# Three two by two pairs in place of two in the first half of a channel mixer, on one Trainium2 core

## The chip, the cores and the metric

The kernel runs on one core of one Trainium2 chip. The metric is the device time of one execution in microseconds, as the median of a few runs of the same kernel. Three runs of the kernel before gave a median of 690.75 us (690.72 to 690.81). The profile is one further execution of that kernel, with its own time.

A core has a matrix engine (TensorE, PE in the profile, with its weight loads in a row of their own, PEld), a vector engine (VectorE, DVE), a scalar engine (ScalarE, ACT), a general engine (GpSimd, POOL) and a queue engine (SyncE, SP) that here only issues transfers. Each engine works through its own list of instructions in order, and semaphores tie the lists together.

## What is computed

The reference is one layer of a hybrid block on 512 positions of width 1024, in float32:

```python
h = rms_norm(x, norm_mix_g);  proj = h @ w_in
# gated short convolution, attention with forgetting, two gates, then
x = x + (g_conv * y_conv + g_attn * y_attn) @ w_o
h = rms_norm(x, norm_ffn_g)
up = causal_dwconv(h @ w_up, conv_ffn_w)      # 1024 -> 2 x 2816, three taps along the positions
a, b = split(up)
x = x + (silu(a) * b) @ w_down                # 2816 -> 1024
return rms_norm(x, norm_f_g)
```

The change lies in `h @ w_up` and its three taps, the channel mixer's way up.

## The kernel before

**Number format.** Each float32 factor is split into a high part and the rest (`wh`, `wl` for weights, `x1h`, `x1l` for the mixer's input), both in a rounded format that TensorE takes at one pass each. A product is three passes: high by high, rest by high, high by rest. Splitting a weight chunk is one copy on ScalarE (L279) and one subtraction on VectorE (L283). `split` does it, and `chunk` hands the next split chunk to the matmuls. Two high and two rest buffers are in use in turn, so a chunk can be split while the one before it is multiplied.

**The mixer in two halves.** The hidden width of 2816 is 22 pairs j of 128 columns of `a` and 128 of `b`. `PHASES` cuts them into a first half (j = 0 to 11) and a second (12 to 21). Each half first computes its pairs (`up`), then multiplies the products by its rows of `w_down` (`down`, L330, tiles `dn`).

**A direct pair** is two blocks (`block`), each 8 slices of the contraction by 3 passes by 2 halves of the positions, 48 matmuls of 256 positions. Its tiles are `p_up`, in one PSUM bank per block; block 2j is `a`, block 2j + 1 is `b`.

**A two by two pair** (`up_pair`, the j in `UPS`) computes both blocks at once with the Strassen-Winograd scheme: seven products of blocks of 128 by 128 in place of eight. Four partial sums lie in four banks, the tiles `us`. Its 84 matmuls take their weights in two steps, each a chunk `P` (768 columns, the plain weights) and a chunk `F` (1024 columns, the weight sums). After them VectorE adds the partial sums up (L1099 to L1104) and scales them by the inverse norm (L1127, L1125).

**Weight sums.** The `F` chunks are sums of weight blocks that transfers make on the chip before they are needed: `group` lists six transfers for a group of two steps, copies on SyncE's queue (L140) and adding transfers on GpSimd's queue (L143), each waiting for the one before. `tick` issues the next of them; `ticks` says how many per split chunk, and `MIXED` says how many groups are interleaved, copy by copy and add by add. The tiles are `sum`. GpSimd's list holds these adds in line with its multiplications.

**After a pair.** `tapped` runs the three taps on each block (one step on ScalarE, L615, two on VectorE, L616 and L619, tiles `fu`; three buffers in turn). `glu` applies SiLU (L1147) and multiplies on GpSimd: an even j gives `ge` (L1150), an odd one `go` (L1157). Both of a couple (2q, 2q + 1) together are then turned into four further sums (L1167 to L1172) and split (L1176 on ScalarE, L1177 on VectorE, tiles `gh`, `gl`) for `down`. These last pieces are queued in `later` and let out behind the splits of later chunks.

**Order.** In the second half the taps of a two by two pair are held (`held_up`) until the next block is multiplied and its successor chunks are split; in the first half they follow the pair at once. `after_split` is the scheduler's constraint that puts an operation behind the latest splits. PSUM banks are handed out by `ring`, a fixed circle of eight numbers; `down` uses the sets X = (6, 7, 0, 1) and Y = (2, 3, 4, 5).

Of the kernel before, what the change touches and what calls it, by code (L numbers as in the profile page):

```python
# [40 lines left out]
PHASES = ((0, 12), (12, NP))  # L41
# [11 lines left out]
)  # L53
GS = 2
NFF = len(STEPS[0]) + len(STEPS[1])
UPS = (3, 7, 12, 15, 18)
NUP = NFF + 2 * (8 - GS)
MIXED = (4, 2, 4, 4, 2, 4, 2)

PLAIN = [(m, k) for m in (6, 7) for k in range(*PHASES[1])]  # L60
PCUTS = (0, 4, 12, 20)
# [3 lines left out]
def block_kernel(ctx, tc, xT, vecs, wv, win, wmix, wo, wup, wst, wdp, outT):  # L65
# [13 lines left out]
    def bank(i, name):  # L79
        return ps.tile([P, S], F32, tag=f"b{i}", name=name)  # L80

    def ring(*ids):
        st = [0]

        def f(name):
            st[0] += 1
            return bank(ids[(st[0] - 1) % len(ids)], name)

        return f
# [32 lines left out]
    for (j0, j1), n0, n1 in zip(PHASES, (0, len(STEPS[0])), (len(STEPS[0]), NFF - 1)):  # L122
        groups += [[NUP + 2 * i, NUP + 2 * i + 1] for i, j in enumerate(UPS) if j0 <= j < j1]
        groups += [list(range(n, min(n + 2, n1))) for n in range(n0, n1, 2)]
    groups.append([NFF - 1])
    nstep = [len(d) for d in STEPS[0] + STEPS[1]] + [2] * (2 * (KB - GS) + 2 * len(UPS))
    todo = []
# [26 lines left out]
    i0 = 0  # L154
    for n in MIXED:
        todo += [op for ops in zip(*map(group, range(i0, i0 + n))) for op in ops]
# [11 lines left out]
    def up_n(j):  # L168
        return [NUP + 2 * UPS.index(j) + d for d in range(2)]

# [13 lines left out]
    n = 0  # L184
    for ph, (j0, j1) in enumerate(PHASES):
        for j in range(j0, j1):
            if j in UPS:
                for m in up_n(j):
# [13 lines left out]
    def after_split():  # L202

        st = ExitStack()
        for ins in order.values():
            st.enter_context(tc.issue_after(ins))
        return st
# [35 lines left out]
    def ticks(nm):  # L243

        if nm[0] in "iw":
            return 2 if nm in ("wo2", "wo4", "wo6") else 1
        if nm[0] == "m":
            return 2
        if nm[0] == "u":
            n = int(nm[2:])  # L250
            return 2 if n > 4 and n % (4 if n >= 2 * PHASES[1][0] else 2) != (3 if n >= 2 * PHASES[1][0] else 1) else 1
        return int(nm[0] == "F" and (int(nm[1:]) % 2 == 1 or int(nm[1:]) >= NUP))

    def split(hl=None):

        k = len(parts)
        if k == len(stream):
            return
        nm, _, ncol = stream[k]
        load(k + (LOOK if k >= gs0 else AHEAD))  # L260
        if k >= gs0:
            for _ in range(ticks(nm)):
                tick()
        if hl is None:
            hl = []
            for x in "hl":
                if k == 0:
                    wp.tile([P, PADW[x]], F32, tag=f"pad{x}", name=f"pad_{x}")
                hl.append(wp.tile([P, D], F32R, tag=f"w{x}", name=f"w{x}_{nm}", bufs=2)[:, :ncol])
        hi, lo = hl  # L270
        raw = raws[k]
        if k < 2:
            if k:
                keep(nc.scalar.activation(hi[:, :VW], raw[:, :VW], AF.Copy))
            else:
                keep(nc.vector.tensor_copy(hi[:, :VW], raw[:, :VW]))
            keep(nc.vector.tensor_copy(hi[:, VW:], raw[:, VW:]))
        else:
            ins = nc.scalar.activation(hi, raw, AF.Copy)  # L279
            order["hi"] = ins.ins  # L280
            if k < KB:
                keep(ins)
        ins = nc.vector.tensor_sub(lo, raw, hi.bitcast(F32))  # L283
        order["lo"] = ins.ins
        if k < KB:
            keep(ins)
        held[0] -= 1
        parts.append((hi, lo))
        run_later(k, 0.45 if nm[0] in "PF" and int(nm[1:]) >= NUP else {"u": 1.7, "P": 1.6, "F": 0.75, "d": 0}.get(nm[0], 3.5))
# [446 lines left out]
    n = 4 * H  # L736
# [59 lines left out]
    acc, bank_s, bank_t = ring(2, 0, 1), ring(3, 4), ring(5, 6)  # L796
# [12 lines left out]
    n = len(units)  # L809
# [21 lines left out]
    acc = ring(3, 4, 5, 6, 0, 1, 2, 7)  # L831
# [137 lines left out]
    def block(name, xh, xl, lead=False):  # L969
        wh, wl = chunk(name)  # L970
        q = acc(f"p_{name}")
        for kb in range(KB):
            ks = slice(kb * P, (kb + 1) * P)
            if lead and kb < 2:
                if kb:
                    passes([
                        (q[:, cs], 0, wh[:, b], wl[:, b], xh[:, a, cs], xl[:, a, cs], True, False)
                        for a, b in enumerate((slice(0, P), ks)) for cs in halves
                    ], 4)
                continue  # L980
            mm3(q, wh[:, ks], wl[:, ks], xh[:, kb, :], xl[:, kb, :], kb == 0, kb == KB - 1)
        return q
# [50 lines left out]
    xf_last.pop()()  # L1033
    nc.vector.tensor_sub(n2[1], ssq2, n2[0].bitcast(F32))
    xf_last.pop()()
    acc = ring(0, 1, 4, 5, 6, 7, 2, 3)
    nrm = {}

    def mid():
# [33 lines left out]
    def fz(name):  # L1073
        fz.n += 2
        a = 2 * KB + fz.n % (2 * KB)
        return xg[:, a : a + 2].rearrange("p h c -> p (h c)")
# [11 lines left out]
    def up_pair(j):  # L1088

        nonlocal xg, x1  # L1090
        flush([("xf", q) for q in range(4)])
        p23, p45, p16, p7 = banks = [acc(f"us{j}{i}") for i in range(4)]
        pair(up_n(j), x1_form, banks)
        z = fp.tile([P, S], F32, tag="fu", name=f"uz{j}", bufs=3)
        u = fp.tile([P, S], F32, tag="fu", name=f"uu{j}", bufs=3)[:, : S // 2]
        lo, hi = halves
        with after_split():
            nc.scalar.activation(z[:, lo], p16[:, lo], AF.Copy)
            nc.vector.tensor_add(z[:, hi], p16[:, hi], z[:, lo])  # L1099
            nc.vector.tensor_add(u, p7[:, lo], z[:, hi])  # L1100
            nc.vector.tensor_add(z[:, hi], p45[:, hi], z[:, hi])
            nc.vector.tensor_add(p23, p23, z)
            p45h = p45.rearrange(halves_of, h=2)
            nc.vector.tensor_add(p45h, p45h, u.unsqueeze(1).to_broadcast([P, 2, S // 2]))  # L1104
        if j == UPS[-1]:
            xg = xfp.tile([P, 4 * KB, 2 * P], F32, tag="xf", name="xg")
            x1 = xg[:, : 2 * KB].rearrange(whole, h=2)
            for a in range(0, KB, 4):
                nc.gpsimd.dma_start(x1[:, a : a + 4, :], x1d[:, a : a + 4, :])
        return p23, p45  # L1110

    def up(ph, j, rb2, pu=None):
        uu = []
        if j in UPS:
            pu = up_pair(j)
        for s_ in range(2):
            p = pu[s_] if pu else block(f"up{2 * j + s_}", x1h, x1l, True)
            if s_ == 0 and held_up:
                while len(parts) < chunk.n + 2:
                    split()  # L1120
                with after_split():
                    held_up.pop()()
            z = p if j <= UPS[-1] else fz(f"fz{j}{s_}")
            if s_ and j in UPS:
                nc.vector.scalar_tensor_tensor(z, p, -1.0, rb2, op0=ALU.mult, op1=ALU.mult)  # L1125
            else:
                nc.vector.tensor_mul(z, p, rb2)  # L1127
            if j not in UPS or not ph:
                z = tapped(j, s_, z)
            uu.append(z)  # L1130
        if j in UPS and ph:
            held_up.append(lambda: glu(ph, j, [tapped(j, s_, z) for s_, z in enumerate(uu)]))
        else:
            glu(ph, j, uu)
# [3 lines left out]
    def tapped(j, s_, z):  # L1138
        u = fp.tile([P, S], F32, tag="fu", name=f"fu{j}{s_}", bufs=3)
        taps(u, z, CF + 3 * (2 * j + s_))  # L1140
        return u
# [171 lines left out]
    for ph, (j0, j1) in enumerate(PHASES):  # L1313
        if ph:
            flush()
            acc = ring(*X, *Y)
        for j in range(j0, j1):
            up(ph, j, nrm["b"], None if j else pu)
        down(ph, ph * len(STEPS[0]))
# [212 lines left out]
```

## Time and profile before

| | |
|---|---|
| median of 3 runs | 690.75 us (690.72 to 690.81) |
| the profiled execution | 690.7 us, span 688.9 us |
| granted TensorE clock | 0.998 |
| TensorE busy | 680.0 us, 99% of the span, 5916 matmuls |
| VectorE busy | 547.3 us, 79% |
| ScalarE busy | 364.6 us, 53% |
| GpSimd busy | 184.2 us, 27% |
| first half, way up | 344.9 to 466.7 us |
| first half, way down | 466.7 to 523.8 us |
| second half, way up | 523.8 to 629.7 us |

Times in the views are microseconds from the span's start. The span is what the profiler saw from the first instruction to the last; the execution's own time is 1.8 us longer. Matmuls are pipelined, so the mean time of one (276 ns) is longer than the distance from one to the next; that distance is read from the chain of work that ended last, which lists a stretch of matmuls with its length and count.

### The profile page before, as it was taken

Reading aid. Unit: us, or ns where it says so; the run is one execution under the profiler, and the core shown is the slowest. Engines: PE = TensorE matmul, PEld = TensorE weight load, DVE = VectorE, ACT = ScalarE, POOL = GpSimd, SP = SyncE. Lnnn points to the kernel's source line nnn. Section 1 sums busy time; section 2 is a strip of 40 time slices with the busy share of each in tenths; the row PEclk is TensorE's granted clock in tenths of the full one; section 3 lists DMA queues with packets and bytes.
Section 4 is the critical chain, followed back from the end, with each engine's and each line's share of the span. In section 5 each row is a group of like instructions: output and inputs, shape, how many; then the busy total and the mean of one; then the engine's idle time right before and its main releaser. Section 6 shows DMA issues by size and latency. Waiting matters only on the chain.

```text
span 688.9 us, 14690 instructions
## 1 busy us (share of the span) xinstructions
PE 680.0 (99%) x5916; PEld 677.8 (98%) x5916; DVE 547.3 (79%) x864; ACT 364.6 (53%) x581; POOL 184.2 (27%) x209
## 2 busy tenths in 40 slices
PE   9999999999999999999999999999999999999996
PEld 8999999999999999999999999999999999999996
DVE  6677777886687877768987989987665889999885
ACT  6575556554564544446654635545444445456563
POOL 5123745444021010233502141330131322222000
PEclk9999999999999999999999999999999999999999
DMA  8626957478579797888985859679799987674623
GB/s 295 208 89 217 198 154 174 100 184 167 131 221 279 214 262 197 240 270 281 213 225 133 227 119 293 156 216 253 219 290 309 251 193 183 187 239 132 188 78 123
DMA packets 66117, 139.64 MB, mean 203 GB/s; under 512 B 5856, under 2 KB 30432, under 8 KB 65792
## 3 DMA queue, kind: packets, MB, share of 16 engines
q1 hardware_dynamic: 44592, 105.72, 46.7%
q0 software_dynamic: 20736, 32.28, 26.9%
q8 instruction: 46, 0.75, 0.4%
q10 hardware_dynamic: 720, 0.69, 0.3%
q14 instruction: 23, 0.19, 0.1%
HBM read 132.32 MB, written 49.81 MB: 264 GB/s over the span
## 4 chain that ended last, share of the span: by engine, by line
PE 89%; DVE 6%; ACT 2%; issue 2%; DMA 1%; ACTq 0%; POOL 0%; SPq 0%; DVEq 0%; POOLq 0%
PE p_up L312 18%; PE p_in L312 14%; PE dn L330 13%; PE gs L330 8%; PE p_wo L312 6%; PE us L330 6%; PE p_up L330 6%; PE yc L330 3%; PE ya L312 3%; PE o L705 2%; PE pa L524 2%; PE pb L526 1%; PE tp L690 1%; PE pdB L312 1%; PE pdA L312 1%
## 5 line engine op out<-in xcount | busy, mean ns | idle before, releaser
L143 POOL DMA_DIRECT2D sum<-in_wst_dram x66 | 70.8, 1163 | 122.3 <-DMA sum<-sum 93.0
L312 PE MATMUL p_in<-xf,wh_in 128*128 128x256 f32 x576 | 95.7, 278 | 0.0
L312 PE MATMUL p_up<-x1h,wh_up 128*128 128x256 f32 x416 | 81.1, 276 | 0.0
L312 PEld LDWEIGHTS p_in<-xf,wh_in 128*128 128x128 f32 x576 | 80.4, 188 | 0.7
L312 PE MATMUL p_up<-x1l,wh_up 128*128 128x256 f32 x416 | 81.0, 276 | 0.0
L312 PE MATMUL p_up<-x1h,wl_up 128*128 128x256 f32 x416 | 80.9, 276 | 0.0
L279 ACT ACTIVATE wh_F<-raw_F 128x1024 fp32r<-128x1024 f32 (+1 forms) x42 | 44.2, 1052 | 66.7 <-PE dn L330 26.2
L283 DVE TENSOR_TENSOR wl_F<-raw_F,wh_F 128x1024 fp32r<-128x1024 f32 (+1 forms) x42 | 53.4, 1272 | 28.8 <-ACT wh_F L279 28.5
L312 PEld LDWEIGHTS p_up<-x1h,wh_up 128*128 128x128 f32 x416 | 62.7, 188 | 0.0
L312 PEld LDWEIGHTS p_up<-x1l,wh_up 128*128 128x128 f32 x416 | 62.6, 188 | 0.0
L312 PEld LDWEIGHTS p_up<-x1h,wl_up 128*128 128x128 f32 x416 | 62.5, 188 | 0.0
L312 PE MATMUL p_in<-xf,wl_in 128*128 128x256 f32 x288 | 56.6, 278 | 0.1
L279 ACT ACTIVATE wh_up<-raw_up 128x1024 fp32r<-128x1024 f32 x34 | 36.0, 1057 | 38.2 <-PE p_up L312 27.9
L279 ACT ACTIVATE wh_P<-raw_P 128x768 fp32r<-128x768 f32 (+1 forms) x42 | 35.1, 836 | 36.4 <-PE dn L330 15.9
L283 DVE TENSOR_TENSOR wl_P<-raw_P,wh_P 128x768 fp32r<-128x768 f32 (+1 forms) x42 | 40.2, 956 | 12.5 <-ACT wh_P L279 6.8
L283 DVE TENSOR_TENSOR wl_up<-raw_up,wh_up 128x1024 fp32r<-128x1024 f32 x34 | 42.3, 1246 | 7.6 <-ACT wh_up L279 7.6
L312 PEld LDWEIGHTS p_in<-xf,wl_in 128*128 128x128 f32 x288 | 43.5, 188 | 0.3 <-DVE wl_in L283 0.3
L1150 POOL TENSOR_TENSOR ge<-fu,fu 128x512 f32<-128x512 f32 x11 | 20.2, 1832 | 67.5 <-DVE fu L619 34.0
L330 PE MATMUL dn<-gh,wh_F 128*128 128x256 f32 x156 | 36.4, 276 | 0.0
L330 PE MATMUL dn<-gl,wh_F 128*128 128x256 f32 x156 | 36.3, 276 | 0.0
L283 DVE TENSOR_TENSOR wl_in<-raw_in,wh_in 128x1024 fp32r<-128x1024 f32 x24 | 30.2, 1258 | 6.1 <-ACT wh_in L279 6.0
L279 ACT ACTIVATE wh_in<-raw_in 128x1024 fp32r<-128x1024 f32 x24 | 25.3, 1056 | 10.8 <-issue 3.4
(361 smaller groups left out, 2106.0 us busy)
## 6 DMA issues: line engine op xcount, KB each, us to landing
raw_F<-sum SPq DMA_DIRECT2D x41, 512.0 KB, 5.4
raw_up<-in_wup_dram SPq DMA_DIRECT2D x34, 512.0 KB, 5.9
raw_P<-in_wst_dram SPq DMA_DIRECT2D x41, 384.0 KB, 4.8
raw_in<-in_win_dram SPq DMA_DIRECT2D x24, 512.0 KB, 3.6
sum<-in_wst_dram POOLq DMA_DIRECT2D x41, 256.0 KB, 6.3
sum<-in_wst_dram SPq DMA_DIRECT2D x20, 512.0 KB, 8.7
sum<-in_wst_dram POOLq DMA_DIRECT2D x20, 512.0 KB, 9.6
sum<-sum SPq DMA_DIRECT2D x40, 256.0 KB, 5.7
```

The lines of the kernel that those rows point to most:

```text
L143: return lambda: keep(nc.gpsimd.dma_start(dst, src, accum_op=ALU.add))
L279: ins = nc.scalar.activation(hi, raw, AF.Copy)
L283: ins = nc.vector.tensor_sub(lo, raw, hi.bitcast(F32))
L312: keep(nc.tensor.matmul(out[:, cs], w, x[:, cs], start=start and i == 0 and c == 0, stop=stop and i == 2 and c == len(cut) - 1,))
L330: keep(nc.tensor.matmul(out, wl if x == 1 else wh, xl if x == 2 else xh, start=opens and bk not in seen, stop=closes and bk not in left,))
L524: keep(nc.tensor.matmul(pa[t][:, :VW], xt, w[:, :VW], start=start, stop=stop))
L526: keep(nc.tensor.matmul(pb[t], xt, w[:, VW:], start=start and t % 2 == 0, stop=stop and t % 2 == 1))
L690: keep(nc.tensor.transpose(tp[:, ks], pt[:, ks], ident))
L705: keep(nc.tensor.matmul(o[:, os_], vv[:, kb, pr, e, :], x[:, kb, cs], start=e == 0 and kb == 0 and i == 0, stop=e == 1 and kb == nk - 1 an ...
L1150: keep(nc.gpsimd.tensor_mul(ge, a.rearrange(halves_of, h=2), b.rearrange(halves_of, h=2)))
```

## The change

The first half gets three two by two pairs, j = 3, 6 and 9, in place of 3 and 7. The second half keeps 12, 15 and 18. There is one weight group more (23 in place of 22), so the interleaving `MIXED` and the number of ticks per chunk are other. The taps of the first half's two by two pairs are held like the second half's. The circle of PSUM banks for the first half puts banks 2 and 3 ahead of 6 and 7.

```diff
-UPS = (3, 7, 12, 15, 18)
+UPS = (3, 6, 9, 12, 15, 18)
 NUP = NFF + 2 * (8 - GS)
-MIXED = (4, 2, 4, 4, 2, 4, 2)
+MIXED = (4, 2, 4, 5, 2, 3, 3)
...
         if nm[0] in "iw":
-            return 2 if nm in ("wo2", "wo4", "wo6") else 1
+            return 2 if nm in ("wo0", "wo2", "wo4", "wo6") else 1
...
             n = int(nm[2:])
-            return 2 if n > 4 and n % (4 if n >= 2 * PHASES[1][0] else 2) != (3 if n >= 2 * PHASES[1][0] else 1) else 1
+            return 2 if n > 2 and n % 4 != 3 else 1
...
-    acc = ring(0, 1, 4, 5, 6, 7, 2, 3)
+    acc = ring(0, 1, 4, 5, 2, 3, 6, 7)
...
-            if j not in UPS or not ph:
+            if j not in UPS:
                 z = tapped(j, s_, z)
             uu.append(z)
-        if j in UPS and ph:
+        if j in UPS:
             held_up.append(lambda: glu(ph, j, [tapped(j, s_, z) for s_, z in enumerate(uu)]))
```

How the lists of instructions stand at three places follows. A row is line, operation, output<-inputs and shape; the number behind a tile's name is the pair and block, the couple q, or the weight group, and the one behind the underscore is the program's own.

First, VectorE behind pair 3 (`fu30`, `fu31` are its taps, `fu40` the taps of the next block, `wl_up10` and `wl_up11` the rests of chunks to come). Before:

```order
L1125 SCALAR_TENSOR_TENSOR us31_4983<-us31_4983,rb_n2_4660 128x512
L1127 TENSOR_TENSOR p_up8_5133<-p_up8_5133,rb_n2_4660 128x512
L616 SCALAR_TENSOR_TENSOR fu30_5117<-us30_4982,vec_64,fu30_5117 128x511
L283 TENSOR_TENSOR wl_up10_5256<-raw_up10_5041,wh_up10_5255 128x1024
L619 SCALAR_TENSOR_TENSOR fu30_5117<-us30_4982,vec_64,fu30_5117 128x510
L616 SCALAR_TENSOR_TENSOR fu31_5122<-us31_4983,vec_64,fu31_5122 128x511
L616 SCALAR_TENSOR_TENSOR fu40_5183<-p_up8_5133,vec_64,fu40_5183 128x511
L619 SCALAR_TENSOR_TENSOR fu31_5122<-us31_4983,vec_64,fu31_5122 128x510
```

Now:

```order
L1125 SCALAR_TENSOR_TENSOR us31_4987<-us31_4987,rb_n2_4662 128x512
L1127 TENSOR_TENSOR p_up8_5122<-p_up8_5122,rb_n2_4662 128x512
L283 TENSOR_TENSOR wl_up10_5188<-raw_up10_5045,wh_up10_5187 128x1024
L616 SCALAR_TENSOR_TENSOR fu30_5191<-us30_4986,vec_64,fu30_5191 128x511
L616 SCALAR_TENSOR_TENSOR fu31_5195<-us31_4987,vec_64,fu31_5195 128x511
L619 SCALAR_TENSOR_TENSOR fu30_5191<-us30_4986,vec_64,fu30_5191 128x510
L619 SCALAR_TENSOR_TENSOR fu31_5195<-us31_4987,vec_64,fu31_5195 128x510
L616 SCALAR_TENSOR_TENSOR fu40_5203<-p_up8_5122,vec_64,fu40_5203 128x511
```

The rest of chunk up10 now stands ahead of all four tap steps of pair 3.

Second, GpSimd in the last third of the first half's way up (`go4` is the product of pair 9, `ge4` of pair 8, `ge5` of pair 10; `sum14` is the group of pair 12 before, `sum15` that of pair 15 before and of pair 12 now, `sum16` that of pair 15 now). Before:

```order
L1157 TENSOR_TENSOR go3_5668<-fu70_5654,fu71_5659 128x512
L1150 TENSOR_TENSOR ge4_5786<-fu80_5720,fu81_5781 128x512
L143 DMA sum14_98<-in_wst_dram 256x1x256
L143 DMA sum15_99<-in_wst_dram 256x1x256
L1157 TENSOR_TENSOR go4_5924<-fu90_5850,fu91_5915 128x512
L143 DMA sum14_98<-in_wst_dram 256x1x256
L1150 TENSOR_TENSOR ge5_6054<-fu100_5984,fu101_6049 128x512
```

Now:

```order
L1157 TENSOR_TENSOR go3_5673<-fu70_5614,fu71_5668 128x512
L143 DMA sum15_99<-in_wst_dram 256x1x512
L143 DMA sum16_100<-in_wst_dram 256x1x512
L1150 TENSOR_TENSOR ge4_5792<-fu80_5725,fu81_5787 128x512
L143 DMA sum15_99<-in_wst_dram 256x1x256
L143 DMA sum16_100<-in_wst_dram 256x1x256
L143 DMA sum15_99<-in_wst_dram 256x1x256
L143 DMA sum16_100<-in_wst_dram 256x1x256
L1157 TENSOR_TENSOR go4_6012<-fu90_6003,fu91_6007 128x512
L1150 TENSOR_TENSOR ge5_6074<-fu100_6015,fu101_6069 128x512
```

All three adds of two groups now lie between `go3` and `go4`. Before, `go4` stood behind the second add of both, and the first adds stood ahead of `go3`.

Third, VectorE ahead of the way down (`wl_P0` is the rest of the first chunk of `down`; `go4` with L1168 to L1172 are the further sums of pairs 8 and 9, `gl` their rests). Before:

```order
L616 SCALAR_TENSOR_TENSOR fu101_6049<-p_up21_5999,vec_64,fu101_6049 128x511
L1177 TENSOR_TENSOR gl_4720<-go4_5924,gh_4719 128x512
L619 SCALAR_TENSOR_TENSOR fu101_6049<-p_up21_5999,vec_64,fu101_6049 128x510
L1177 TENSOR_TENSOR gl_4720<-go4_5924,gh_4719 128x512
L1127 TENSOR_TENSOR p_up22_6068<-p_up22_6068,rb_n2_4660 128x512
L283 TENSOR_TENSOR wl_P0_6192<-raw_P0_5926,wh_P0_6191 128x768
```

Now:

```order
L619 SCALAR_TENSOR_TENSOR fu101_6069<-p_up21_6019,vec_64,fu101_6069 128x510
L1168 TENSOR_TENSOR go4_6012<-go4_6012,ge4_5792 128x256
L1127 TENSOR_TENSOR p_up22_6076<-p_up22_6076,rb_n2_4662 128x512
L1171 SCALAR_TENSOR_TENSOR go4_6012<-go4_6012 128x256
L1177 TENSOR_TENSOR gl_4722<-ge4_5792,gh_4721 128x256
L1172 SCALAR_TENSOR_TENSOR go4_6012<-go4_6012 128x256
L616 SCALAR_TENSOR_TENSOR fu110_6126<-p_up22_6076,vec_64,fu110_6126 128x511
L1177 TENSOR_TENSOR gl_4722<-go4_6012,gh_4721 128x512
L619 SCALAR_TENSOR_TENSOR fu110_6126<-p_up22_6076,vec_64,fu110_6126 128x510
L1177 TENSOR_TENSOR gl_4722<-go4_6012,gh_4721 128x512 x2
L283 TENSOR_TENSOR wl_P0_6208<-raw_P0_5908,wh_P0_6207 128x768
```

The further sums of pairs 8 and 9 and all four of their rests now stand between the taps of block 21 and `wl_P0`; before, `wl_P0` came right behind the last of these rests, with the further sums well ahead of them.

## The prediction

> **What bounds the kernel now.** I read the page's busy times first, then what TensorE waits for, then the chain of work that ended last.
>
> ```profile
> span 688.9 us, 14690 instructions
> PE 680.0 (99%) x5916; PEld 677.8 (98%) x5916; DVE 547.3 (79%) x864; ACT 364.6 (53%) x581; POOL 184.2 (27%) x209
> ```
>
> TensorE is busy for 99% of the span: time can only be won by fewer matmuls or by ending one of its few waits. Its waits, all of them:
>
> ```profile
> PE warm L108 <- DVE ones L100: 1.1, 1, 1.1
> PE us L330 <- DVE wl_P L283: 0.9, 1, 0.9
> PE pa L524 <- ACT wh_v L274: 0.4, 1, 0.4
> ```
>
> Two belong to the start. The third, 0.9 us (name, total, times, longest), is a two by two pair that waits for VectorE's rest of its first chunk, `wl_P`. The chain (start, length, what, count) shows where that is:
>
> ```profile
> 366.02 1.36 PE p_up L330 x12
> 367.38 4.08 PE p_up L312 x36
> 371.46 9.52 PE us L330 x84
> ...
> 413.62 9.52 PE us L330 x84
> ...
> 466.67 57.12 PE dn L330 x504
> ...
> 588.65 8.45 PE us L330 x72
> ```
>
> The first half runs from pair 3 (371.46) into `down` (466.67) without a gap. The wait ends at 588.65, where only 72 of 84 matmuls follow: it stands in pair 18, behind its 12 matmuls with the high part.
>
> **The change, part by part.**
>
> *Matmuls.* A block of 48 takes 1.36 + 4.08 = 5.44 us, 0.1133 each; a two by two pair of 84 takes 9.52, also 0.1133 each. A direct pair is two blocks, 10.88 us. One more pair is changed over: 12 matmuls and **1.36 us** less.
>
> *Work of the other engines.* The stage's totals (columns: stretch, its length, busy of PE, PEld, DVE, ACT, POOL, clock, DMA share):
>
> ```profile
> 344.90:466.70 121.80, 121.80 (x1076) 121.80 (x1076) 105.56 (x148) 60.89 (x87) 33.63 (x26) 1.00 0.75 196
> 523.80:629.70 105.90, 104.96 (x926) 104.76 (x926) 95.52 (x136) 52.53 (x77) 30.33 (x27) 1.00 0.77 212
> ```
>
> ```profile
> L283 DVE TENSOR_TENSOR wl_up<-raw_up,wh_up 128x1024 fp32r<-128x1024 f32 x18 | 21.9, 1215 | 3.7 <-ACT wh_up L279 3.7
> L283 DVE TENSOR_TENSOR wl_F<-raw_F,wh_F 128x1024 fp32r<-128x1024 f32 x4 | 6.6, 1650 | 1.7 <-ACT wh_F L279 1.7
> L283 DVE TENSOR_TENSOR wl_P<-raw_P,wh_P 128x768 fp32r<-128x768 f32 x5 | 4.7, 950 | 0.2 <-DMA raw_P<-in_wst_dram 0.2
> L1102 DVE TENSOR_TENSOR us<-us,uz 128x512 f32<-128x512 f32 x2 | 1.4, 700 | 0.1
> L1099 DVE TENSOR_TENSOR uz<-us,uz 128x256 f32<-128x256 f32 x2 | 0.8, 418 | 0.0
> ```
>
> VectorE gets two `wl_P` and two `wl_F` for two `wl_up`, 2 x 0.95 + 2 x 1.65 - 2 x 1.22 = 2.8 us, and five additions, three like L1099 and two like L1102, 2.7: some 5.5 us more. It was idle for 121.8 - 105.6 = 16.2 us there, so on average this hides behind the matmuls; without that cover it would cost up to 5.5. ScalarE idles half the stage. The extra weight group is 1 MB of copies and 1 MB of adds in a stage whose transfer share is 0.75; by the table of ticks the last add of any group now comes at least 6 chunks before its chunk is loaded. I cost these at nothing, as I do the other bank circle: four banks per two by two pair and four per two direct pairs close the circle of eight, so `down`'s first set, (6, 7, 0, 1), is last used by pair 9, whose taps end before its product can start, 9 us before `down` by the model below.
>
> *Spacing.* What matters is when VectorE falls behind. Pairs 3, 6, 9 and then `down` (four blocks between each) have the spacing of 15 and 18 in the second half, held taps included, so that stretch is the model for the new one:
>
> ```profile
> 563.46 0.42 DVE L1167 TENSOR_TENSOR go<-ge 128x256 f32<-128x256 f32 x1
> ...
> 564.93 1.22 DVE L283 TENSOR_TENSOR wl_up<-raw_up,wh_up 128x1024 fp32r<-128x1024 f32 x1
> ...
> 566.39 0.68 DVE L1177 TENSOR_TENSOR gl<-ge,gh 128x512 fp32r<-128x512 f32 x1
> ...
> 579.86 0.75 DVE L616 SCALAR_TENSOR_TENSOR fu<-p_up,vec,fu 128x511 f32<-128x511 f32 x1 [0.26 <-ACT fu L615]
> ...
> 580.86 0.74 DVE L619 SCALAR_TENSOR_TENSOR fu<-p_up,vec,fu 128x510 f32<-128x510 f32 x1
> ...
> 582.11 1.22 DVE L1168 TENSOR_TENSOR go<-go,ge 128x256 f32<-128x256 f32 x1
> ...
> 587.64 0.95 DVE L283 TENSOR_TENSOR wl_P<-raw_P,wh_P 128x768 fp32r<-128x768 f32 x1
> ```
>
> Counted from the first matmul of pair 15, the next `wl_P` is needed after 9.52 + 4 x 5.44 + 12 x 0.1133 = 32.64 us. The wait ended at 588.65 and took 0.9, so it was needed at 587.7, and pair 15 began at 555.1. `wl_P` was ready at 588.6, 33.5 after. In the first half the even couple's rest is a smaller operation:
>
> ```profile
> 379.86 0.42 DVE L1177 TENSOR_TENSOR gl<-ge,gh 128x256 fp32r<-128x256 f32 x1
> ```
>
> 0.42 for 0.68, twice in such a stretch: 0.5 us less. Before pair 6 one set of four further sums is missing as well (563.46 to 564.93, 1.5 us), so its `wl_P` is ready 31.5 after pair 3 begins: no wait, 1.1 to spare. Between 9 and `down` both sets are there: ready at 33.0 for 32.6, **a wait of 0.4 us** at the first step of `down`. Pair 18's own 0.9 stays, as that stage keeps its work.
>
> *Adds in GpSimd's list.* Now three adds of two groups stand between `go3` and `go4`, and the taps of block 21 use a buffer that `go4` has to read first. In the model, the same multiplication is the one at 577.22:
>
> ```profile
> 559.74 1.29 POOL L1150 TENSOR_TENSOR ge<-fu,fu 128x512 f32<-128x512 f32 x1 [9.01 <-issue]
> ...
> 577.22 1.30 POOL L1157 TENSOR_TENSOR go<-fu,fu 128x512 f32<-128x512 f32 x1 [5.08 <-DVE fu L616]
> ```
>
> It starts 22.1 after pair 15 begins and VectorE already idles 0.26 for it (579.86 above). Pair 9 begins at 371.46 + 2 x 31.28 = 434.0; with the smaller rest `go4` is due at 455.9, and each us later makes `wl_P0` a us later. Before it come, each started by the landing of the one before: the first adds, a copy, the second adds, a copy, the third adds. From 400 to 470 these took (KB, median us to landing):
>
> ```profile
> sum<-in_wst_dram POOLq DMA_DIRECT2D x8, 256.0 KB, 5.8
> ...
> sum<-in_wst_dram POOLq DMA_DIRECT2D x3, 512.0 KB, 10.2
> ...
> sum<-sum SPq DMA_DIRECT2D x4, 256.0 KB, 3.5
> ```
>
> The chain starts behind `go3`. Its last input, the model's 580.86 + 0.74 = 26.5 after pair 15 begins, less 0.6 for one operation that is missing there (a quarter of the 1.5 above) and the smaller rest, comes 25.9 after pair 6 begins (402.7), at 428.7; it ends at 430.0. The later first add starts 0.6 behind: 430.6 + 10.2 + 3.5 + 5.8 + 3.5 = 453.6, and 0.6 for the last issue: 454.2, 1.7 us before `go4` is due. So by medians it costs **nothing**. Nothing here shows a gain below that. The dear end: two first adds issued together when transfers were denser (466 to 524),
>
> ```profile
> L143 POOL DMA_DIRECT2D sum<-in_wst_dram x2: 1676/1697/1718, 500.7 to 501.7; - x2
> ...
> DMA to landing us min/median/max: 13.0/14.8/16.7
> ```
>
> and the page's medians for the rest:
>
> ```profile
> sum<-in_wst_dram POOLq DMA_DIRECT2D x41, 256.0 KB, 6.3
> ...
> sum<-sum SPq DMA_DIRECT2D x40, 256.0 KB, 5.7
> ```
>
> 430.6 + 16.7 + 5.7 + 6.3 + 5.7 + 0.6 = 465.6, 9.7 too late. I take the near end, since its rows are from this stage, and keep the other for the range.
>
> The Trainium skill (DMA: Bandwidth & Descriptors, "Anatomy of one DMA — SWDGE (gpsimd) path") gives a GpSimd transfer 2.0 us plus its bytes over 436 GB/s, by which an add of 512 KB would land in an estimated 3.2 us and one of 256 KB in 2.6. By it the chain would end ten us earlier and `go4` could not be late; the sum would be the same. The rows say 10.2 and 5.8, two to three times as long, so I do not lean on it.
>
> *Sum.* From the profiled execution's 690.7 (span 688.9 and 1.8 around it; the median of the runs is 690.75, the same): 690.7 - 1.36 + 0.4 = **689.7 us**.
>
> **Rivals.**
>
> *The adds come late.* As above: SyncE's copy waits for an add, GpSimd's next add for the copy, `go4` stands behind, then block 21's taps, then `wl_P0`, then `down`. For it: the margin of 1.7 us is less than the spread of one landing. Against it: medians of this stage. From 0.96 us of delay the gain is gone; from 2.4 it is slower by more than 0.2%. Halfway between the ends, some 4 us late: 693.7; at the dear end 699.4. The Trainium skill (SBUF — State Buffer, "SBUF: two separate sides") adds a reason: VectorE and GpSimd share a pair of ports as a lock, and a VectorE operation can keep GpSimd from writing a transfer's descriptors. No row here separates that from other delay.
>
> *VectorE becomes the bound.* It has 92% after the change ((105.6 + 5.5) of 120.4). If none of the 5.5 us hides: 690.7 - 1.36 + 5.5 = 694.8. Against it: it catches up, idle before pairs 3 and 9, in the model as here.
>
> *A wait goes.* Pair 18's 0.9 us hangs on some tenths: `L1168` took 1.22 for its usual 0.42 because GpSimd multiplied beside it. With other transfers in GpSimd's list that could shift; without it and without the 0.4: 690.7 - 1.36 - 0.9 = 688.4. With the new wait alone absent, 689.3.
>
> *The change does nothing.* Excluded: 12 matmuls go from an engine that is 99% busy.
>
> **How the numbers follow.** A measurement tells about 0.2%, 1.4 us, from no change; the whole cut in matmuls is 1.36, just under it. Forecast, cut less a small wait (689.4 to 690.4): 0.42, no change. Adds late by 0.7 to 2.4 us: 0.13, no change; later: 0.16, slower. VectorE the bound: 0.05, slower. A wait gone or none made: 0.24, faster. So faster 0.24, same 0.55, slower 0.21. The range, 688.8 to 692.3, leaves out the lowest part of the last case and the adds late by more than 2.6.
>
> **What would show it.** TensorE: 5904 matmuls, three rows of 84 at 9.52 in the first half. A wait of `dn` for `wl_P` of some 0.4; well above that, the add rival, if GpSimd's `go4` starts after 456 behind an add that waited for `sum<-sum`. Pair 6 without a wait; if `us` waits there, VectorE is the bound. Pair 18's wait again at 0.9. I am wrong if TensorE waits for a bank or for a raw chunk, or if the distance of matmuls is another.

## The result and the profile after

The changed kernel takes 695.41 us (median of 4 runs, 694.78 to 697.47) against 690.78 (690.72 to 690.92) for the kernel before on the same chip: a ratio of 1.0072, 95% interval 1.0051 to 1.0093. It is **slower by 0.7%**, where no change was forecast at 689.7, and outside the range of 688.8 to 692.3. The profiled execution of it took 695.23 us, with a span of 693.5, that of before 688.9; the ledger below is made between these two spans.

The page's busy times, and the waits of TensorE (name, total, times, longest):

```profile
span 693.5 us, 14700 instructions
PE 681.1 (98%) x5904; PEld 678.5 (98%) x5904; DVE 551.0 (79%) x871; ACT 365.8 (53%) x584; POOL 184.8 (27%) x212
```

```profile
PE dn L330 <- DVE wl_P L283: 3.0, 1, 3.0
PE us L330 <- DVE wl_P L283: 0.9, 1, 0.9
PE dn L330 <- ACT wh_F L279: 0.2, 1, 0.2
```

The 12 matmuls are gone (5904 for 5916). Yet TensorE's busy time went up, from 680.0 to 681.1: some of the matmuls that are left run longer. The chain of waits (start, length, what, count) shows which ones, and what TensorE waits for:

```profile
372.06 9.52 PE us L330 x84
...
430.40 8.78 DMA sum<-in_wst_dram
439.19 4.01 DMA sum<-sum
443.75 7.23 DMA sum<-in_wst_dram
451.00 5.26 DMA sum<-sum
470.23 57.54 PE dn L330 x492
527.77 9.52 PE us L330 x84
...
635.97 33.94 PE dn L330 x297
```

In the kernel before, the chain holds nothing but TensorE between pair 3 and the way down. Now the transfers of two weight groups stand in it: first add, copy, second add, copy. And the 492 matmuls of `down` take 57.54 us, where at 0.1133 each they would take 55.74: 1.8 us more. Here is the end of that stretch in the same chain, taken closer:

```profile
457.83 1.52 POOL sum L143
459.35 1.32 POOL go L1157
...
461.24 0.68 ACT fu L615
...
462.01 0.75 DVE fu L616
...
469.31 0.88 DVE wl_P L283
```

GpSimd issues the two last adds, then multiplies `go4` (459.35), ScalarE may then begin the taps of block 21, VectorE goes on with them, and eight microseconds of queued VectorE work later `wl_P` is ready and `down` starts. VectorE had stood still for `go4`:

```profile
462.01 0.75 DVE L616 SCALAR_TENSOR_TENSOR fu<-p_up,vec,fu 128x511 f32<-128x511 f32 x1 [3.19 <-ACT fu L615]
```

And this is TensorE around the wait (stretch, its length, busy PE and its matmuls, granted clock, transfer share, GB/s):

```profile
467.00:468.00 1.00, 0.26 (x3) 1.00 0.57 49
...
469.00:470.00 1.00, 0.00 (x0) 1.00 0.91 125
470.00:471.00 1.00, 0.77 (x3) 0.51 0.85 154
471.00:472.00 1.00, 1.00 (x7) 0.50 0.96 195
...
473.00:474.00 1.00, 1.00 (x8) 0.78 0.83 245
474.00:475.00 1.00, 1.00 (x11) 1.00 0.77 250
```

TensorE is idle from 467.26. At 470 the granted clock falls to half, just as the matmuls come back; they run at 7 in a microsecond for 11, until about 473.4. So the wait costs twice: 3.0 us of idleness and 1.8 us behind it. The low clock is not all of the 1.8. In two runs below the same 492 matmuls come behind a wait while the clock stays at 1.00, and they take 56.06 us (the row is shown there). So some 0.3 is lost by starting again after the wait, and some 1.5 by the low clock: from 470.23 to 473.4 the matmuls come every 0.21 us in place of every 0.11.

**The ledger** between the spans (+4.6): from pair 3 (371.46 before, 372.06 now) to the first pair of the second half (523.78 and 527.77) 152.32 us have become 155.71. That is +3.39, made of -1.36 for the matmuls, +3.0 for the wait and +1.8 behind it. Ahead of it pair 3 begins 0.6 later. Behind it some 0.6 are lost. The new wait for `wh_F` accounts for 0.5 of that: 0.2 us of waiting, and 0.3 for starting again (297 matmuls at 0.1133 would be 33.65 us, and the chain has 33.94). These two small losses were forecast by no step; the experiments below find both.

### The profile page after: what moved, and what is told of

Read it like the earlier page. It is cut to its first block, busy times and chain, and to the rows that moved or that the text cites. A ratio compares the mean times of both kernels' runs of the same rounds, so it can differ in the third digit from the quotient of the medians.

```text
span 693.5 us, 14700 instructions
## 1 busy us (share of the span) xinstructions
PE 681.1 (98%) x5904; PEld 678.5 (98%) x5904; DVE 551.0 (79%) x871; ACT 365.8 (53%) x584; POOL 184.8 (27%) x212
## 4 chain that ended last, share of the span: by engine, by line
PE 68%; DVE 16%; DMA 5%; ACT 5%; issue 4%; POOL 1%; ACTq 0%; SPq 0%; DVEq 0%; POOLq 0%
PE p_in L312 14%; PE dn L330 13%; PE p_up L312 9%; PE gs L330 8%; PE us L330 5%; DMA sum<-in_wst_dram 3%; PE yc L330 3%; PE ya L312 3%; PE p_up L330 2%; DVE wl_up L283 2%; DVE gl L1177 2%; DVE fu L616 2%; PE pa L524 2%; PE pb L526 2%; DVE fu L619 2%
## 5 line engine op out<-in xcount | busy, mean ns | idle before, releaser
L143 POOL DMA_DIRECT2D sum<-in_wst_dram x69 | 73.7, 1257 | 123.7 <-DMA sum<-sum 85.4
L283 DVE TENSOR_TENSOR wl_F<-raw_F,wh_F 128x1024 fp32r<-128x1024 f32 (+1 forms) x44 | 56.9, 1293 | 30.3 <-ACT wh_F L279 30.1
L312 PE MATMUL p_up<-x1h,wl_up 128*128 128x256 f32 x392 | 76.4, 276 | 0.1
L312 PE MATMUL p_up<-x1h,wh_up 128*128 128x256 f32 x392 | 76.4, 276 | 0.0
L312 PE MATMUL p_up<-x1l,wh_up 128*128 128x256 f32 x392 | 76.3, 276 | 0.0
L312 PEld LDWEIGHTS p_up<-x1h,wl_up 128*128 128x128 f32 x392 | 59.0, 188 | 0.3 <-DVE wl_up L283 0.3
L312 PEld LDWEIGHTS p_up<-x1h,wh_up 128*128 128x128 f32 x392 | 59.1, 188 | 0.0
L312 PEld LDWEIGHTS p_up<-x1l,wh_up 128*128 128x128 f32 x392 | 59.0, 188 | 0.0
L283 DVE TENSOR_TENSOR wl_up<-raw_up,wh_up 128x1024 fp32r<-128x1024 f32 x32 | 39.9, 1248 | 5.5 <-ACT wh_up L279 5.4
L1150 POOL TENSOR_TENSOR ge<-fu,fu 128x512 f32<-128x512 f32 x11 | 17.4, 1579 | 81.6 <-ACT fu L1147 40.4
```

What stands on the lines that cost most here:

```text
L143: return lambda: keep(nc.gpsimd.dma_start(dst, src, accum_op=ALU.add))
L312: keep(nc.tensor.matmul(out[:, cs], w, x[:, cs], start=start and i == 0 and c == 0, stop=stop and i == 2 and c == len(cut) - 1,))
L1150: keep(nc.gpsimd.tensor_mul(ge, a.rearrange(halves_of, h=2), b.rearrange(halves_of, h=2)))
```

## The experiments

The theory after the result: `go4` stands in GpSimd's list behind adds that wait for copies, is late, and TensorE pays for the lateness and then for the low clock. The rivals: VectorE's own backlog from 5.5 us more work; a low clock with a cause of its own; the held taps; the banks. In each pair of times below the second is the kernel before on the same chip.

### The two last adds behind go4

```diff
-            return 2 if n > 2 and n % 4 != 3 else 1
+            return {22: 0, 23: 3}.get(n, 2 if n > 2 and n % 4 != 3 else 1)
```

> The changed kernel with one line other: the last adds of weight groups 15 and 16 are issued one chunk later, behind GpSimd's product go4 of pair 9 and the next even one, in place of ahead of both. Theory (go4 stands behind an add that waits for a copy, 2.6 us more than by medians; TensorE then idles 3.0 us and runs slower for some microseconds after): go4 starts at 456 +-0.7, VectorE's 3.2 us wait for the tap's first half is gone, the first step of down waits 0 to 0.5 for its weights' rest, the 492 matmuls of down take 55.7 to 55.9 in place of 57.5, the clock stays above 0.9 there, and the time is 690.3 (689.7 to 690.9): 695.4 less 3.0 less 1.8 less up to 0.4. Rival, VectorE's own backlog (5.5 us more work): the wait stays at 2.5 to 3 and the time at 694.5 to 695.5. Rival, the low clock has another cause than the wait: the wait goes, down still takes 57.5, 692.3.

691.05 us (690.42 to 692.41) against 690.85: ratio 1.0006 (0.9997 to 1.0015). GpSimd's timeline, first of the changed kernel, then of this one:

```profile
457.27 2.08 POOL L143 DMA_DIRECT2D sum<-in_wst_dram  x2 [7.39 <-DMA sum<-sum]
458.40 2.27 POOL L1157 TENSOR_TENSOR go<-fu,fu 128x512 f32<-128x512 f32 x1
```

```profile
455.59 1.30 POOL L1157 TENSOR_TENSOR go<-fu,fu 128x512 f32<-128x512 f32 x1 [6.09 <-ACT fu L1147]
...
461.52 3.17 POOL L143 DMA_DIRECT2D sum<-in_wst_dram  x3
```

`go4` now waits for its own input and ends at 456.9 in place of 460.7. The chain of waits has the three pairs and the whole of `down` without a gap:

```profile
371.68 9.52 PE us L330 x84
...
402.96 9.52 PE us L330 x84
...
434.24 9.52 PE us L330 x84
...
465.52 57.12 PE dn L330 x504
522.64 9.52 PE us L330 x84
...
631.37 33.95 PE dn L330 x297
```

From pair 3 to the second half it is 150.96 us, 1.36 less than the 152.32 before: exactly the matmuls. No wait, no low clock, and 504 matmuls at 0.1133. So the theory holds for the 4.8 us, and VectorE's backlog as their cause is refuted: its work is the same here. The time missed the expected span (689.7 to 690.9) by a little, and the gain of 1.36 still isn't there. Most of it went at the second `down`, where a wait has grown from nothing in the kernel before:

```profile
PE dn L330 <- ACT wh_F L279: 0.7, 1, 0.7
```

### The product of pair 9 on VectorE

```diff
-            keep(mul(nc.gpsimd))
+            keep(mul(nc.vector if j == 9 else nc.gpsimd))
```

> The changed kernel with the product go4 of pair 9 alone on VectorE in place of GpSimd: the adds stay where they were and stay late, but nothing that the way down needs stands behind them. Theory (queue position behind the adds): VectorE gets about 0.7 us more, loses the 3.2 us wait; the first step of down waits 0 to 1.0; no low clock; 690.8 (690.0 to 691.4). Rival, VectorE's backlog: 0.7 longer than the changed kernel, 696. Rival, low clock of another cause: 692.5.

691.31 us (690.83 to 693.45) against 690.85: 1.0012 (1.0003 to 1.0021). The adds stay where they are, but nothing that `down` needs stands behind them: its wait for `wl_P` is 0.6 us, the clock stays at 1.00, and the 492 matmuls behind the wait take 56.06. A second way out of the same queue gives the same relief, so it was the queue and not the number or the moment of the transfers.

### More lateness, with no transfer in it

Two and four more copies of the same product ahead of `go4`, in the kernel with the adds behind (here two):

```diff
+            for _ in range(2 if j == 9 else 0):
+                keep(nc.gpsimd.tensor_mul(go[:, 0:2, :], ...))
             keep(mul(nc.gpsimd))
```

> The kernel with the adds behind go4, and ahead of go4 two more copies of the same product on GpSimd (same inputs, overwritten by the real one), some 1.3 us each, so go4 ends about 2.6 later with no DMA in it. Theory (any lateness of go4 goes to TensorE one to one once VectorE's idle time is used up, and an idle TensorE of some 3 us costs about 1.8 more by the clock behind it): the wait at the first step of down is 2 to 3.1, down takes 57 to 57.6, time 693.5 to 695.3. Rival, no link between wait and clock: 692.3 to 693.2, down 55.8. Rival, go4 has slack and the lateness hides: 690.5.

> The kernel with the first half's last adds behind go4 (691.05), and ahead of go4 four more copies of the same product on GpSimd, some 1.3 to 1.6 us each. With two of them TensorE idled 2.6 us at the first step of down and its clock stayed at 1.00 in the profiled run; in the changed kernel it idled 3.0 us and the clock stood at 0.51 for some 3.4 us. Theory (a threshold between 2.6 and 3.0 us of idle TensorE, and behind it a fixed time at half the clock): the wait is 5 to 6 us, the clock is 0.5 for 3 to 4 us, the 492 matmuls of down take 57.4 to 57.8, time 697.3 to 699. Rival, the low clock's length grows with the idle time: down takes 58.5 or more, 699 to 701. Rival, the low clock in the changed kernel was not from the wait: down 56.1, 696 to 697.

With two: 694.21 us (693.32 to 695.07) against 690.85, as expected. But the profiled run, the quickest of them, waits 2.6 us, and its clock does not fall, where a low clock had been expected:

```profile
469.00:470.00 1.00, 0.14 (x1) 1.00 1.25 200
470.00:471.00 1.00, 1.00 (x9) 1.00 1.24 176
```

```profile
469.86 56.06 PE dn L330 x492
```

The slowest of its four runs (695.07) has a mean clock of 0.994, as the changed kernel has, and the other three 0.996 or 0.997; whether its clock fell at the wait is in no trace.

With four: 699.29 us (698.32 to 699.65) against 690.62, just above the 697.3 to 699 expected. The wait is 5.2 us, and the clock falls while TensorE is still idle:

```profile
467.00:468.00 1.00, 0.37 (x4) 1.00 0.00 0
...
470.00:471.00 1.00, 0.00 (x0) 0.70 0.89 132
...
477.00:478.00 1.00, 1.00 (x9) 0.88 1.03 202
```

```profile
472.57 58.33 PE dn L330 x492
```

A clock of 0.70 in a stretch is 0.4 of it at full and 0.6 at half. So the clock fell at 470.4, 3.0 us after the last matmul, and came back at 477.24 (0.88: 0.24 at half), 6.8 us later. `down` lost 58.33 - 55.74 = 2.6 us, 0.3 of it for starting again and 2.3 by the clock. My theory of a fixed 1.8 was too small, the rival of a length that grows with the wait (58.5 or more) a little too large; what the traces show is in the last section. From two copies to four, `go4` ends 2.8 us later (463.65 for 460.89) and the wait grows by 2.6. That lateness of `go4` goes to TensorE nearly one to one, and that a long enough wait then costs again, is shown with no add in the way.

### The taps and the banks

The kernel before with the held taps and the new bank order alone; the kernel with the adds behind, once without the hold and once with the old banks:

```diff
-            if j not in UPS or not ph:
+            if j not in UPS:
...
-        if j in UPS and ph:
+        if j in UPS:
...
-    acc = ring(0, 1, 4, 5, 6, 7, 2, 3)
+    acc = ring(0, 1, 4, 5, 2, 3, 6, 7)
```

> The kernel before (pairs 3 and 7 two by two, its own ticks) with only the two smaller parts of the change: taps of the first half's pairs held until a later split, and the banks of the way up in the other order. Theory: both cost nothing here, 690.75 +-0.4, no wait of TensorE but the three of before. Rival, the hold or the banks make part of the loss: a wait of us, p_up or dn for a bank or a weight rest, 691.5 or more.

> The kernel with the first half's last adds behind go4 (691.05), with the taps of the first half's three pairs run at once again, as before the change, in place of behind a later split. Theory (with two blocks of direct pairs between, the hold costs what it cost alone, a median of 1.4 at pairs 3 and 7, by a late rest of the weights): faster, 689.8 to 690.6. Rival, the hold costs nothing at this spacing and brings nothing: 690.8 to 691.3. Rival, without the hold 2.8 us of taps stand ahead of the next rest of weights: p_up waits 1 to 2.5 behind each pair, 692 to 697.

> The kernel with the first half's last adds behind go4 (691.05), with the banks of the way up in the order of before. With three pairs the circle then ends on banks 6 and 7, the first that down opens, in place of 2 and 3. Theory (the bank order matters only for who holds down's first banks): dn waits for VectorE's scaling of block 23 and its taps, which end some 2 to 5 us after the block's last matmul, time 693 to 698, with a lower clock if the wait is 3 us. Rival, the order costs nothing either way: 690.8 to 691.3.

Alone: 692.25 us (691.64 to 693.21) against 690.85, 1.0018 (1.0009 to 1.0027). No cost was expected; the rival, 691.5 or more, holds. That part is not free at the old spacing, and which of the two it is, the hold or the banks, was not tried there. The profiled run, again the quickest, has one new wait of TensorE's weight loads behind pair 7:

```profile
PEld p_up L330 <- DVE wl_up L283: 0.3, 1, 0.3
```

That covers a third of a microsecond; where the rest of the median goes was not in a profile and stays open.

Without the hold: 692.71 us (692.40 to 694.93) against 690.62, so some 1.9 slower than with it, each taken against the kernel before beside it. Between pairs 6 and 9 TensorE waits for a weight rest that stands behind the taps (and that takes 1.95 us there for its usual 1.22):

```profile
PE p_up L330 <- DVE wl_up L283: 1.1, 1, 1.1
```

At the new spacing the hold is needed. My expectation that undoing it would help was wrong: what it costs beside pairs 3 and 7 says nothing on pairs 3, 6 and 9.

With the old banks: 696.99 us (696.10 to 697.32) against 690.62. The circle then ends on banks 6 and 7, which `down` opens first, and it waits for the taps of block 23:

```profile
PE dn L330 <- DVE fu L619: 3.9, 1, 3.9
```

So the third pair needs the new bank order, and costing that order at nothing was right.

### The second half: the load of x1

In the kernel with the adds behind, the second `down` loses 1.0 us: the wait of 0.7 and 0.3 for starting again (33.95 for 33.65). ScalarE stands there for the load of `x1` (timelines of ScalarE and VectorE):

```profile
609.04 0.42 ACT L1358 ACTIVATE gh<-xg 128x256 fp32r<-128x256 f32 x1 [3.74 <-DMA xg<-x1d]
```

```profile
613.61 0.75 DVE L616 SCALAR_TENSOR_TENSOR fu<-xg,vec,fu 128x511 f32<-128x511 f32 x1 [1.94 <-ACT fu L615]
```

Behind it are pair 18's activation, its product on GpSimd, the taps, and at last `wh_F`. The load itself is longer than it was (KB, median us to landing; the kernel before, then the one with the adds behind):

```profile
xg<-x1d POOLq DMA_DIRECT2D x2, 1024.0 KB, 8.9
```

```profile
xg<-x1d POOLq DMA_DIRECT2D x2, 1024.0 KB, 10.9
```

The change cuts the groups of weight sums differently (2, 3, 3 at the end of the table for 2, 4, 2), so adds of other groups are in flight there. First one of them was moved behind the load and the next products, then all three:

```diff
-            return {22: 0, 23: 3}.get(n, ...)
+            return {22: 0, 23: 3, 39: 0, 40: 0, 42: 3, 43: 2}.get(n, ...)
```

```diff
-            return {22: 0, 23: 3}.get(n, ...)
+            return {22: 0, 23: 3, 38: 0, 39: 0, 40: 0, 41: 3, 42: 3, 43: 3}.get(n, ...)
```

> The kernel with the first half's last adds behind go4 (691.05), and one more edit in its second half: the second add of the last weight group, one of three adds that were in flight while x1 is loaded back, is issued behind pair 18's even product and pair 19's product, and the last copies and adds a chunk or two later. In the kernel without this edit the load of x1 landed 9.7 and 12.2 us after its issue (7.8 and 10.0 in the kernel before, with two adds about it), ScalarE stood 3.7 us for it, VectorE 1.9 for ScalarE, and the second down waited 0.7 for wh_F with 0.3 of lower rate behind. Theory (the third add makes the load late, the lateness goes down that chain): the load lands by 607.5, the wait of dn for wh_F falls to 0 to 0.2, time 690.1 (689.6 to 690.5). Rival, the chain of VectorE's own work sets it (TensorE comes 1.1 us sooner and nothing else does): the wait stays 0.6 to 0.9, time 691.0. Rival, the copies that now stand in SyncE's list ahead of weight loads make a new wait: over 692.

> The kernel with the first half's last adds behind go4 (691.05), and in its second half all three second adds of the last groups (the largest 256 KB) issued behind the load of x1 and the two next products, their copies and last adds after them. Moving one of the three (690.95) left the load at 9.3 and 11.8 us and the wait of the second down for wh_F at 0.4. Theory (the adds of the last groups, not that one alone, make the load of x1 land late, ScalarE stands for it, and the second down waits): the load takes 7.5 to 8.5 and 9.5 to 10.5 us, the wait of dn for wh_F is gone, time 689.6 to 690.3. Rival, the weight loads that TensorE asks for 1.1 us sooner make it late: the load stays at 9.3 and 11.8, the wait at 0.4 to 0.7, 690.8 to 691.1.

One moved: 690.95 us (690.04 to 692.66) against 690.62, where 689.6 to 690.5 was expected, with the load at 10.6 and the wait at 0.4. That theory fell: it was not the one add. All three moved: 690.48 us (690.13 to 691.35) against 690.80, 0.9997 (0.9988 to 1.0005), a little above the 689.6 to 690.3 expected. The load is down to

```profile
xg<-x1d POOLq DMA_DIRECT2D x2, 1024.0 KB, 7.8
```

and the wait for `wh_F` is gone. In the two later kernels with the same adds moved it takes 8.4 and 9.4, and 10.4 to 11.1 in seven traces with all of them in place. So it was the adds and copies of the last groups together that stretched the load. The rival, weight loads that TensorE asks for sooner, is refuted, since these are still there.

### The 0.9 us of pair 18, and the start of the way up

In the kernel with no adds at the load, and in the kernel before:

```diff
+        if j == 17 and len(parts) == chunk.n:
+            split()
         flush()
         ge = glu.even
```

> As the run with no adds at the load of x1, and one more line: in the second half the rest of pair 18's first weight chunk (wl_P, 0.95 us) is made ahead of pair 17's taps and the last sums of the pair before, in place of behind them. It aims at the 0.9 us that TensorE waits there in the kernel before and in every version so far. Theory (that wait is VectorE's order, the weights are long there): the wait of us for wl_P goes, nothing else comes in its place, 1.0 to 1.1 us less (0.9 and the refill behind it) than the run with no adds at the load, so 688.5 to 689.3 and faster than the kernel before by 1.5 to 2.2. Rival, what is put behind comes late next (the product of pairs 16 and 17, the next rest of weights): a wait of p_up for wl_up of 0.5 to 1, no gain.

> The kernel before with that last line alone: the rest of pair 18's first chunk ahead of pair 17's taps. Theory: its 0.9 us wait goes as well, 689.6 to 689.9, so that the third two by two pair by itself is worth the difference to the run with the same line in the changed kernel, 0.5 to 1.2 us, at most the 1.36 of its matmuls. Rival: the second down then waits more for wh_F, as TensorE comes a us sooner and the load of x1 does not: 690.3 to 690.9.

689.58 us (688.69 to 690.59) against 690.80, 0.9984 (0.9975 to 0.9993), above the 688.5 to 689.3 expected; in the kernel before 689.78 (689.13 to 692.30), 0.9990 (0.9982 to 0.9999). The wait goes in both, so it was only the order in VectorE's list, and each gains about 1 us by it. But with this line the change brought 0.2 us and not 1.36. Part of what was left is ahead of pair 3. There VectorE's short operations are caught beside GpSimd's product `L946`; of the two rows the first is the kernel before, the second the changed one:

```profile
308.86 1.76 DVE L990 TENSOR_TENSOR xs<-xs 128x256 f32<-128x256 f32 x1
```

```profile
309.92 2.29 DVE L994 SCALAR_TENSOR_TENSOR xs<-xs 128x256 f32<-128x256 f32 x1
```

Each takes 0.42 by itself. The change puts one more add ahead of GpSimd's loads at chunk `wo0`, so the product comes later (310.08 for 308.50) and VectorE is done later. Which operation is held differs from run to run: with no adds at the load of `x1` it is `L993` (2.36), with `L990` and `L994` at 0.42. The last run gives that step to `wo3`:

```diff
-            return 2 if nm in ("wo0", "wo2", "wo4", "wo6") else 1
+            return 2 if nm in ("wo2", "wo3", "wo4", "wo6") else 1
```

> As the run with pair 18's rest first (689.58), and the extra step of weight sums that the change puts at chunk wo0 put at wo3, so that GpSimd's list through the output projection is that of the kernel before. In the changed kernels so far VectorE's operation L990 or L994 of 0.42 us took 2.07 to 2.29 there beside GpSimd's product L946, 1.76 in the kernel before, and the first blocks of the way up waited 0.1 to 0.5 us for wl_up, with 0.0 in the kernel before. Theory (GpSimd's product comes late behind the added transfer and takes VectorE's time): the wait at 338 is gone, 689.1 (688.6 to 689.5), so that the three pairs with all the shifted waits removed are worth 0.5 to 1.1 us against the kernel before with pair 18's rest first (689.78). Rival, the 0.1 to 0.5 us at 338 are of the adds in flight: the wait stays, 689.4 to 689.7.

689.11 us (688.79 to 689.90) against 690.75: 0.9979 (0.9970 to 0.9988). `L990` is back at 1.76 and nothing waits at 338. In its profiled run 0.5 us of the wait for `wh_F` came back, so that one is not settled for good. This version beats both kernels. Against the kernel before with pair 18's line the ratios stand 0.0011 apart, some 0.8 us; their intervals overlap a little, and the moved adds were not tried in the kernel before. So that this share is the third pair's is likely, not proved.

## Why the prediction was wrong

*Matmuls, -1.36.* Right: 5904, three rows of 84 at 9.52, and exactly 1.36 between pair 3 and the second half wherever nothing waits.

*The wait of 0.4 at the first step of down.* Mis-sized. With the adds behind `go4` (first experiment), `wl_P` was ready 32.3 us after pair 9 began at 434.24, where the model said 33.0 and 32.6 was the limit: no wait, 0.36 to spare.

```profile
465.57 0.95 DVE L283 TENSOR_TENSOR wl_P<-raw_P,wh_P 128x768 fp32r<-128x768 f32 x1
```

VectorE's added work does hide, pair 6 did not wait and pair 18's 0.9 stayed, all as forecast. That work was put too high at 5.5 us: over the whole kernel VectorE's busy time rose by 3.7 (551.0 for 547.3), and by 2.8 in the kernel with the adds behind (550.1).

*Adds in GpSimd's list, "by medians it costs nothing".* **This is the step that failed.** The place, the chain and what stands behind it were right, as the rival "the adds come late" had them, and given 0.29. The durations were not. The first add took 8.8 for 10.2, but the copies took 4.0 and 5.3 for 3.5 and the second add 7.2 for 5.8. GpSimd began the next issue 0.55 and 1.0 us after the copies had landed, where the sum had no term, and the two last issues took 2.1 us of GpSimd for 0.6. So `go4` could start at 459.35 and not at the 454.2 of the sum. How late that is, the kernel with the adds behind shows: its `go4` started at 455.59, which is 455.97 when moved by the 0.38 us that its pair 3 begins sooner. So `go4` was 3.4 late; 0.36 of that was to spare, and the rest is the wait of 3.0. A margin of 1.7 us behind four transfers in a row was costed at nothing because four medians were added; the row quoted for the dear end had shown 13.0 to 16.7 us for one of them.

*The rival's price.* It counted a late `go4` one to one (4 us late: 693.7). What follows the wait, the low clock above all, was in no step, and adds 1.8 us for 3.0 us of wait. No wait in the trace of before shows it: past the start TensorE's longest there is 0.9 us, with no fall behind it. Only the end of that trace does. TensorE's last matmul ends at 682.68, and 4.0 us later, at 686.64, the clock falls to half (0.82: 0.64 at full):

```profile
686.00:687.00 1.00, 0.00 (x0) 0.82 1.09 384
```

The Trainium skill has it as well (TensorE: Matmul & The Clock Gate, "Why this matters for your kernels"): no idle gap over some 3 us, else the matmuls fall to half rate. The trace agrees at a wait of 3.0 us. With the 3.0 and 1.8 measured here, the rival would have had 689.3 + 3.0 + 1.8 = 694.1, and with the two small losses (0.6 each) 695.3, against 695.23 for the profiled execution.

*The extra group "at nothing".* Wrong in two small places: the load of `x1` went from 8.9 to 10.4 us behind adds of other groups (0.5 at the second `down`, and 1.0 in the kernel with the adds behind), and GpSimd's product came later beside VectorE's sums (0.1 to 0.5 at the start of the way up). Neither showed as a wait of TensorE before, and I had looked only at whether the sums are ready in time, not at what else lies in the queues that they pass.

*The other rivals.* VectorE as the bound is refuted by the first run. "A wait goes" was possible but did not come by itself: the 0.9 us went only when its order was changed. "Does nothing" was rightly excluded.

## What to carry to other kernels

When work is moved into an engine's list behind transfers that wait for one another, add up the slow ends of their landings, not their medians: the margin has to be larger than the spread of the whole chain. A stall of the main engine costs more than itself (here 0.3 us behind each wait, and 1.5 or more besides where the clock fell), so price it with what follows. And a small cut on the critical engine is worth only what the next waits leave of it: here two small ones, 0.1 to 1 us each, took most of 1.36 us even with the large one removed, and a gain over the kernel before showed only when the waits beside them were moved too.

## What the runs showed of the hardware

*The clock of an idle TensorE.* Waits of 0.9 us (pair 18) and 2.6 us (the run with two more products) left the granted clock at 1.00. In the changed kernel it fell to 0.5 at 470.02, some 2.75 us after the last matmul, and stayed there for 3.4 us. With four more products it fell at 470.40, after 3.0 us, and stayed for 6.8. With the old banks:

```profile
466.00:467.00 1.00, 0.39 (x4) 1.00 1.24 198
...
468.00:469.00 1.00, 0.00 (x0) 0.92 1.06 166
...
475.00:476.00 1.00, 1.00 (x8) 0.67 0.21 70
```

it fell at 468.84, 2.45 us after the last matmul (0.92: 0.16 at half), and came back at 475.66, 6.8 us later. So the low clock came in lengths of 3.4 us, once or twice, and the idle time before it varies.

There is an order in when it falls. At the end of the program, where TensorE has no more work, the clock falls once more; in the changed kernel at 688.48:

```profile
688.00:689.00 1.00, 0.00 (x0) 0.74 0.17 62
```

That is 64 times 3.413 us after its first fall. In the run with four more products the two falls (470.40 and 695.69) lie 66 times 3.413 us apart, in the one with the old banks (468.84 and 690.71) 65 times, all to within 0.04 us. So in these runs the clock is set at moments 3.413 us apart that go on whatever the kernel does, and what counts is how much of the stretch before such a moment was idle. Idle times of 2.45, 2.75 and 3.0 us were enough. With two more products the clock falls at 687.24 at the end; 64 steps before that is 468.79, 1.5 us into the wait, and the clock stayed at 1.00. Between 1.5 and 2.45 us lies the limit for these matmuls, by an estimate from these four runs. (At the end of the program 1.3 us after the last matmul was enough, but there the matmuls just before have only 1 or 128 columns.) By these figures, whether a wait of some 2.6 us costs the clock depends on where it lies between two such moments. The clock came back at the first such moment with hardly any idleness in the stretch before it: 0.2 us of it in the changed kernel were little enough, 1.4 with the old banks and 2.2 with four more products were not, and there the half rate went on for a second stretch.

The Trainium skill (TensorE: Matmul & The Clock Gate, "What's actually happening") has a free-running window of 3.4 us, and half rate after at least one idle window. The length and the free run agree; that a whole window of 3.4 us has to be idle does not: 2.45 us of idleness were enough.

*VectorE beside GpSimd.* An operation of 0.42 us took 1.76 to 2.54 over the runs when GpSimd's product `L946` (1.84 us) ran: it did not run slower so much as wait for the product's end. The Trainium skill (SBUF — State Buffer, "SBUF: two separate sides") calls it an exclusive lock, held for the whole instruction. The rows agree: in the changed kernel the product ended at 311.92 and the operation at 312.21. The operation is recorded as starting 0.16 us before the product there, so which of the two came first these rows do not settle.
